# A decoder layer in split fp32: moving the streamed operands to the low end of the partition and the weights to its top

## The chip, the cores and the metric

One core of one Trainium2 chip runs the whole kernel. The metric is device microseconds of one execution. The profile is of one execution of the kernel before; its times are in microseconds from the first instruction.

In the profile PE is TensorE's matmuls, PEld its weight loads, DVE is VectorE, ACT is ScalarE, POOL is GpSimd and SP is SyncE, which issues most DMAs. A matmul's **stationary** operand (128×128 here) is loaded into the array first; its **moving** operand (128×512 here) is then streamed through it. A row such as `pj<-u,w_hi` names the result, then the moving operand, then the stationary one. SBUF has 224 KiB in each partition, and a tile's **place** is where its bytes begin in every partition, counted from the low end.

## The reference, cut to what is computed

```python
def layer(x, c, positions, ...):                 # x [1, 1024, 1024], d_model 1024, fp32
    mod = silu(c) @ w_ada + b_ada                # six vectors: shift, scale, gate, twice
    u = x * (1 + scale_m) + shift_m
    qa, ka, va, qb, kb, vb, ga, gb = split(u @ w_in)     # w_in is 1024 x 7936
    ya = window_attention(rope(qa), rope(ka), va, sinks) @ w_branch_a   # 16 heads, 2 kv heads
    yb = dilated_attention(rope(qb), rope(kb), vb)       @ w_branch_b   # 3 dilations x 8 heads
    y = (sigmoid(ga) * ya + sigmoid(gb) * yb) @ w_o
    x = layer_norm(2**0.25 * x + (1 + gate_m) * y)
    v = x * (1 + scale_f) + shift_f
    g, h = split(v @ w_gate_up)                  # d_ff 2816
    return layer_norm(2**0.25 * x + (1 + gate_f) * ((silu(g) * h) @ w_down))
```

## The kernel before, in words

**Arithmetic.** Each fp32 operand of the large products is held as two exact parts, high and low. `mac` (L130) makes one product of a 128×128 weight tile with 512 columns out of three matmuls: `w_hi` with the high part (L131), `w_hi` with the low part (L132), `w_lo` with the high part (L133). `matmul(ps, w, m)` takes the stationary operand first and the moving one second.

**Weights.** The class `Weights` streams them in pieces of 512 columns through the pool `wpool` (L98): a DMA into `w_raw`, sometimes a scale, then ACT makes `w_hi` (L72) and DVE `w_lo` (L73). Some pieces go into tiles of their own instead (`pair_dest`, L167): the second half of the output projection (`late`, tiles `o_hl` of pool `opar`) and the down projection (`wd` in pool `ffn`, the last one `wdl` in pool `last`). `split` (L110) does the same to an array: ACT makes the high part (L111), DVE the low part (L112).

**Stages, in the order of the program.** A manual schedule keeps the order in which the program is written as the issue order on each engine.

1. 0 to 70 us: the adaLN vectors, `u`^T (in `bigu`, eight tiles of 8 KiB), the rope's tables, and the first three projections, whose stationary operands are tiles `e_hi` and `e_lo` of the pool `pro` (`first_macs`, L271 and L276).
2. 70 to 828 us: the other projections `pj<-u,w` into which the attention is woven. `rotary` (L406) turns a projection: DVE L415 makes `ra`, L416 `rb`, L419 the sum into a tile `o` for queries and `r` for keys; `q_stacks` makes `qs` from `o` (L432 and L433), `k_stacks` makes `kh` and `kl`. Scores are L497, transposes of the probabilities L535, the sums with the values L556, and their result is copied into a tile `o` by ACT (L558). Pool `att` holds all of these; `o` has four buffers for queries and for results. The results of window attention are scaled (L607) and stored to DRAM (`oa_d`, L608); for the last pair of heads (p=7) both are done by POOL (`side`, L601), for the others by DVE and SP.
3. 828 to 1120 us: for two branches of four pairs of heads from `w_branch_a` and one from `w_branch_b`, the gate `p<-u,w` and the product `p<-o_hl,w`. `o_parts` (L788) reads back the stored heads, four tiles a branch: SP loads `o_raw` (L784, two buffers) and `split` makes `o_hl` (four buffers in `opar`).
4. 1120 to 1230 us: the output projection from the merged array `m` (in `bigu` again): `p<-w,m` for the first half of the features with `m` stationary, `pf<-o_hl,m` for the second half, whose weights are the `late` tiles. Then a layer norm and the FFN's input `v` (`ffn_input`, L996): token half t=0 in the pool `u2p` (L988), t=1 in `bigu`.
5. 1230 to 1960 us: the FFN, in groups of two columns of 128: `pf<-v,w` for gate and up, `h` in `bigu`, and `pd<-wd,h` with `h` stationary and `wd` moving.
6. The last layer norm and the stores.

**Places.** A pool takes its space from the low end, or from the top with `side="right"`, and gives it back when it closes. A tile that comes to lie where earlier tiles lay waits for everything that wrote or read them; this is how a place becomes a wait, on the engine that first writes the new tile.

Of the kernel before, what the change touches and what calls it, by code (L numbers as in the profile page):

```python
# [10 lines left out]
F32 = mybir.dt.float32  # L11
# [7 lines left out]
P = 128  # L19
# [21 lines left out]
class Weights:  # L41
    """Streams weights in pieces of 512 columns: DMA, an optional scale, and two exact parts."""
# [15 lines left out]
    def step(self):  # L58
        """Splits the next piece and sends for the one that fits behind it."""
        i = len(self.done)  # L60
        if i >= len(self.jobs):
            return
        self.send()
        _, kh, scale, dest = self.jobs[i]
        raw = self.raws.pop(i)
        if scale is not None:
            self.nc.gpsimd.tensor_tensor(raw, raw, scale(), op=OP.mult)  # L67
        if dest is None:
            hi, lo = [self.pool.tile([P, 512], F32R, name=s, tag=s, bufs=4) for s in ("w_hi", "w_lo")]
        else:  # L70
            hi, lo = dest()
        self.nc.scalar.activation(hi, raw, AF.Copy)  # L72
        self.nc.vector.tensor_tensor(lo, raw, hi, op=OP.subtract)  # L73
        self.done.append((hi, lo, kh))
        self.send()

    def prepare(self, pieces):
        """Sees to it that the next pieces are split."""
        while len(self.done) < min(self.used + pieces, len(self.jobs)):
            self.step()  # L80

    def take(self, pieces):
        """The next pieces, as a function from the chunk to its two parts."""
        self.prepare(pieces)
        got = self.done[self.used:self.used + pieces]
        self.used += pieces
        kh = got[0][2]
        n = 512 // kh
        return lambda k: [got[k // kh][s][:, (k % kh) * n:(k % kh + 1) * n] for s in range(2)]
# [3 lines left out]
def decoder_layer(ctx: ExitStack, tc: tile.TileContext, I, out, dbg=None):  # L93
# [4 lines left out]
    wpool = ctx.enter_context(tc.tile_pool(name="wpool", bufs=2))  # L98
# [15 lines left out]
    # silu(c), one value per partition and chunk of the contraction  # L114
# [6 lines left out]
    def wide(name, pool, halves=(0, 1)):  # L121
        """A [128, 8, 1024] array in two exact parts: a function of part, token half and chunk."""
        ts = {(s, t, k): pool.tile([P, 4, TH], F32R, name=f"{name}{s}{t}{k}", tag="big")
              for t in halves for k in range(2) for s in range(2)}
        return lambda s, t, k: ts[s, t, k // 4][:, k % 4]
# [41 lines left out]
    def pair_dest(store, key, pool, name, bufs):  # L167
        def dest():
            if key not in store:
                store[key] = [pools[pool].tile([P, 2, D], F32R, name=name, bufs=bufs), 0]  # L170
            hl, c = store[key]
            store[key][1] += 1
            return hl[:, 0, c * 512:(c + 1) * 512], hl[:, 1, c * 512:(c + 1) * 512]
        return dest

    for eh in range(2):
        for kp in range(4):
            add_chunk(I["w_o"][eh, kp], 2, 1, lambda eh=eh: gates[2][:, eh * 512:(eh + 1) * 512],
                      pair_dest(late, kp, "opar", "o_hl", 4) if eh else None)
    for f in range(NF):  # L180
        add_chunk(I["w_gate_up"][f], 2, 4)
        add_chunk(I["w_gate_up"][NF + f], 2, 4)
        for c in range(2):
            ws.add(I["w_down"][f * P:(f + 1) * P, c * 512:(c + 1) * 512], 1,
                   lambda c=c: gates[5][:, c * 512:(c + 1) * 512],
                   pair_dest(wd_t, f, "ffn", "wd", 3) if f < NF - 1 else pair_dest(wd_t, f, "last", "wdl", 1))
# [23 lines left out]
    early = {}  # L210
    with tc.tile_pool(name="pro", bufs=2) as pro:
# [14 lines left out]
        # shift and scale of all the chunks, as columns of one bank  # L226
        ps_m = ps_t.tile([P, TH], F32, name="pt")

        def ada_sum(j):
            """Products of the adaLN weights with silu(c), summed over the later chunks."""  # L230
            acc_t[j] = pro.tile([P, 2 * P], F32, name="acc", bufs=2)
            k0 = on_pe[j]
            nc.vector.tensor_scalar(acc_t[j], wa_t[j][:, k0], c_act[:, k0:k0 + 1], None, op0=OP.mult)
            for k in range(k0 + 1, KC):
                nc.vector.scalar_tensor_tensor(acc_t[j], wa_t[j][:, k], c_act[:, k:k + 1], acc_t[j],
                                               op0=OP.mult, op1=OP.add)
# [27 lines left out]
        def first_macs(j):  # L264
            """What the j-th chunk of u^T brings to the first projections, in pieces."""
# [18 lines left out]
        def table_steps():  # L284
            """The rope's angles, reduced to [-pi, pi] (cosines as sines of a quarter turn less the angle's size)."""
# [68 lines left out]

    att = ph1.enter_context(tc.tile_pool(name="att", bufs=2, side="right", reuse_waits="tile"))
    mask_a, mask_b = mask[:, 0:3:2], mask[:, 1:3]

# [44 lines left out]
    def residue_half(ap, r, t):  # L402
        """The places of token half t in an array ordered by the residue modulo r."""
        jn = TH // r
        return ap.rearrange("p (r j) -> p r j", r=r)[:, :, t * jn:(t + 1) * jn]

    def rotary(e, r, then):
        """Rotated features, tokens in the order of their residue modulo r."""
        res = att.tile([P, T], F32, name="o", bufs=4) if e == 2 else att.tile([P, T], F32, name="r", bufs=1)
# [17 lines left out]
    def q_stacks(e, r, box):  # L427
        """Per head [q_hi; q_lo], the leading part on the head's own partitions."""
        def stack(res, h):
            own, other = ((LO, HI), (HI, LO))[h]  # L430
            q = att.tile([P, T], F32R, name="qs", bufs=4)
            nc.scalar.activation(q[own], res[own], AF.Copy)  # L432
            nc.vector.tensor_tensor(q[other], res[own], q[own], op=OP.subtract)  # L433
            box.setdefault("q", []).append(q)
# [7 lines left out]
    def k_stacks(e, r, both, box):  # L442
        """Per head [k_hi; k_hi] and k_lo, on the head's own partitions or on both halves."""
        def stack(res, h):
            own, other = ((LO, HI), (HI, LO))[h]
            kh = att.tile([P, T], F32R, name="kh", bufs=4)
# [18 lines left out]
    def values(e, r, box):  # L465
        """Values [key in block, block, feature], tokens in the order of their residue modulo r."""
# [17 lines left out]
    def scores(un, half, h):  # L484
        """Scaled and masked scores of four blocks of a head, and their maxima, negated."""
# [53 lines left out]
    def weigh(un, half):  # L539
        """Sums of the values for four blocks of both heads."""  # L540
# [9 lines left out]
        if half == 0:  # L550
            un["o"] = att.tile([P, T], F32, name="o", bufs=4)
# [25 lines left out]
    def keep_sums(un):  # L577
        """The reciprocal sums of A's exponentials, the sinks' among them."""
# [22 lines left out]
    def side(p):  # L601
        """The last pair's end keeps to the engine that has nothing else to do then."""
        return (nc.gpsimd, nc.gpsimd) if p == A_PAIRS - 1 else (nc.sync, nc.vector)
# [95 lines left out]
    def tasks(n, i):  # L699
        """What follows the attention of earlier units."""  # L700
# [63 lines left out]
    zp = ctx.enter_context(tc.tile_pool(name="zp", bufs=2, reuse_waits="tile"))  # L764
    misc = ctx.enter_context(tc.tile_pool(name="misc", bufs=1, reuse_waits="tile"))
    ph2, ph2b = ExitStack(), ExitStack()
    opar = ph2.enter_context(tc.tile_pool(name="opar", bufs=4, side="right", reuse_waits="tile"))
    pools["opar"] = opar
# [19 lines left out]
    def o_parts(b):  # L788
        parts = []
        for k in range(4):  # L790
            send_parts(4 * b + 4)
            hl = opar.tile([P, 2, T], F32R, name="o_hl")
# [122 lines left out]
    def moments(tb):  # L915
        """The mean and, still as a variance, the scale of each row."""
# [7 lines left out]
    def norm_quick(tb, gb, dst=None):  # L924
        """z = (z - mean) * gain / sigma + bias for each row of z [128, 1024]."""
# [9 lines left out]
    def norm_shared(tb, gb, dst):  # L935
        """The same with the work spread over three engines, the end as a function to call later."""
# [51 lines left out]
    u2p = ctx.enter_context(tc.tile_pool(name="u2p", bufs=4, reuse_waits="tile"))  # L988
# [7 lines left out]
    def ffn_input(t, dc):  # L996
        if t not in u2:
            u2[t] = wide("v", u2p if t == 0 else bigu, (t,))
# [34 lines left out]
    ph2.close()  # L1033
# [4 lines left out]
    groups = [2] * 9 + [4]  # L1038
    ffn = ctx.enter_context(tc.tile_pool(name="ffn", bufs=2, side="right", reuse_waits="tile"))
    pools["ffn"] = ffn  # L1040
# [11 lines left out]
    for gi, n in enumerate(groups):  # L1052
# [3 lines left out]
        for f in fs:  # L1056
            h = bigu.tile([P, 2, T], F32R, name="h", tag="big")
# [16 lines left out]
            if f == 0:  # L1074
# [5 lines left out]
                pools["last"] = ctx.enter_context(tc.tile_pool(name="last", bufs=1, reuse_waits="tile"))  # L1080
# [32 lines left out]
def _layout(a):  # L1113
    """The arrays as the kernel reads them: reordered only."""
# [67 lines left out]
```

## Time and profile before

| what | value |
|---|---|
| three runs | 1974.82, 1977.31 and 1979.35 us, median 1977.31 |
| the profiled execution, first to last instruction | span 1974.0 us; the profile gives no other time of it |
| PE busy | 1925.3 us (98%), 9252 matmuls |
| DVE, ACT, POOL busy | 1088.3 (55%), 678.5 (34%), 390.5 (20%) |
| mean granted TensorE clock | 0.995 |
| PE idle, 0 to 70 us | 17 us |
| PE idle, 70 to 828 us | 12 us |
| PE idle, 828 to 1120 us | 3 us |
| PE idle, 1120 to 1230 us | 2 us |
| PE idle, 1230 to 1960 us | 7 us |
| PE idle, 1960 to 1974 us | 8 us |

The idle times are each stretch less PE's busy time in it. How to read it: matmuls are pipelined, so one matmul's duration (some 390 ns) is longer than the distance from its start to the next one's start (some 230 ns), and it is the distance that adds up to the span. Starts are read from the timeline; the granted clock is 1.00 at full speed.

### The profile page before, as it was taken

How to read it: one execution, taken by the hardware profiler on the slowest of the kernel's cores; microseconds unless marked ns; L12 is line 12 of the kernel's file. 1: busy time of each engine (PE TensorE's matmuls, PEld its weight loads, DVE VectorE, ACT ScalarE, POOL GpSimd, SP SyncE). 2: the span in 40 equal slices, each digit the busy share in tenths (PEclk: the TensorE clock that was granted, in tenths of full speed). 3: DMA queues.
4: the chain of work that ended last, by engine and by line, in shares of the span. 5: the costliest groups of instructions: out<-in, count | busy, mean ns of one | idle time of the engine just before them, and what ended most of it. 6: DMA issues, size and time to landing. Idle time of an engine off the chain costs nothing.

```text
span 1974.0 us, 24286 instructions
## 1 busy us (share of the span) xinstructions
PE 1925.3 (98%) x9252; PEld 1548.0 (78%) x9252; DVE 1088.3 (55%) x2111; ACT 678.5 (34%) x1501; POOL 390.5 (20%) x259
## 2 busy tenths in 40 slices
PE   6899999999999999999999999999999999999998
PEld 5688878878878777778888878787778777877886
DVE  8755567677676877435454558434433343334337
ACT  3555444445445677532121314211121112111222
POOL 2422223323332222001211333000010001000013
PEclk9899999999999999999999999999999999999999
DMA  8011111121121212355442242111111111111112
GB/s 311 22 38 39 36 59 54 39 66 49 34 72 43 89 65 70 126 180 166 160 144 80 62 131 70 54 54 42 39 59 43 43 43 65 38 38 54 54 48 86
DMA packets 68518, 146.16 MB, mean 74 GB/s; under 512 B 12529, under 2 KB 13617, under 8 KB 68402
## 3 DMA queue, kind: packets, MB, share of 16 engines
q1 hardware_dynamic: 68066, 143.56, 22.2%
q8 instruction: 73, 1.20, 0.3%
q0 software_dynamic: 336, 1.06, 0.2%
q14 instruction: 43, 0.35, 0.1%
HBM read 132.69 MB, written 11.89 MB: 73 GB/s over the span
## 4 chain that ended last, share of the span: by engine, by line
PE 84%; DVE 9%; ACT 2%; DMA 2%; issue 2%; POOL 1%; SPq 0%; DVEq 0%; ACTq 0%
PE pf L132 9%; PE pf L131 9%; PE pf L133 9%; PE pj L131 7%; PE pj L133 7%; PE pj L132 7%; PE p L132 5%; PE p L133 5%; PE p L131 5%; PE pd L131 4%; PE pd L133 4%; PE pd L132 4%; PE s L497 3%; PE pt L535 2%; PE po L556 2%
## 5 line engine op out<-in xcount | busy, mean ns | idle before, releaser
L131 PE MATMUL pj<-u,w_hi 128*128 128x512 f32 x720 | 300.8, 418 | 0.0
L73 DVE TENSOR_TENSOR w_lo<-w_raw,w_hi 128x512 fp32r<-128x512 f32 x238 | 198.9, 845 | 174.9 <-ACT w_hi L72 171.8
L133 PE MATMUL pj<-u,w_lo 128*128 128x512 f32 x720 | 283.3, 393 | 0.0
L132 PE MATMUL pj<-u,w_hi 128*128 128x512 f32 x720 | 282.0, 392 | 0.0
L131 PE MATMUL pf<-v,w_hi 128*128 128x512 f32 x704 | 276.5, 393 | 0.0
L132 PE MATMUL pf<-v,w_hi 128*128 128x512 f32 x704 | 276.2, 392 | 0.0
L133 PE MATMUL pf<-v,w_lo 128*128 128x512 f32 x704 | 275.7, 392 | 0.0
L67 POOL TENSOR_TENSOR w_raw<-w_raw,gate 128x512 f32<-128x512 f32 x60 | 81.8, 1369 | 637.6 <-DMA w_raw<-in_w_down 436.2
L418 POOL TENSOR_TENSOR rb<-rb,sin_t 128x512 f32<-128x512 f32 x64 | 86.9, 1357 | 510.3 <-DVE rb L416 359.7
L519 ACT ACTIVATE probs<-probs,st 128x128 f32<-128x128 f32 (+1 forms) x320 | 146.0, 460 | 53.6 <-DVE st L513 26.6
L1096 DVE SCALAR_TENSOR_TENSOR zt<-zt,pd 128x512 f32<-128x512 f32 x160 | 109.3, 688 | 99.4 <-PE pd L133 99.4
L131 PEld LDWEIGHTS pj<-u,w_hi 128*128 128x128 f32 x720 | 135.9, 189 | 33.5 <-issue 4.9
L133 PEld LDWEIGHTS pj<-u,w_lo 128*128 128x128 f32 x720 | 135.5, 188 | 30.7
L1068 ACT ACTIVATE sg<-pf 128x512 f32<-128x512 f32 x44 | 26.3, 597 | 384.2 <-PE pf L133 384.2
L131 PEld LDWEIGHTS pf<-v,w_hi 128*128 128x128 f32 x704 | 131.9, 187 | 30.2
L133 PEld LDWEIGHTS pf<-v,w_lo 128*128 128x128 f32 x704 | 131.9, 187 | 30.2
L72 ACT ACTIVATE w_hi<-w_raw 128x512 fp32r<-128x512 f32 x238 | 144.5, 622 | 32.0 <-PE p L132 12.5
L132 PEld LDWEIGHTS pf<-v,w_hi 128*128 128x128 f32 x704 | 132.0, 187 | 29.8
L132 PEld LDWEIGHTS pj<-u,w_hi 128*128 128x128 f32 x720 | 136.2, 189 | 22.4
L131 PE MATMUL pd<-wd,h 128*128 128x512 f32 x336 | 133.5, 397 | 6.7 <-DVE zt L1096 6.7
L133 PE MATMUL pd<-wd,h 128*128 128x512 f32 x336 | 133.2, 396 | 0.0
L132 PE MATMUL pd<-wd,h 128*128 128x512 f32 x336 | 132.6, 395 | 0.0
(211 smaller groups left out, 3303.8 us busy)
## 6 DMA issues: line engine op xcount, KB each, us to landing
w_raw<-in_w_in SPq DMA_DIRECT2D x118, 256.0 KB
w_raw<-in_w_gate_up SPq DMA_DIRECT2D x88, 256.0 KB
a_raw<-in_w_ada SPq DMA_DIRECT2D x32, 512.0 KB
w_raw<-in_w_down SPq DMA_DIRECT2D x44, 256.0 KB
wa<-in_w_ada_m SPq DMA_DIRECT2D x16, 512.0 KB
wb<-wt_d SPq DMA_DIRECT2D x24, 256.0 KB
xt<-in_xT SPq DMA_DIRECT2D x8, 512.0 KB
w_raw<-in_w_branch_a SPq DMA_DIRECT2D x16, 256.0 KB
```

What stands on the lines that cost most here:

```text
L67: self.nc.gpsimd.tensor_tensor(raw, raw, scale(), op=OP.mult)
L72: self.nc.scalar.activation(hi, raw, AF.Copy)
L73: self.nc.vector.tensor_tensor(lo, raw, hi, op=OP.subtract)
L131: nc.tensor.matmul(ps, w[0], m[0], start=first, stop=False)
L132: nc.tensor.matmul(ps, w[0], m[1], start=False, stop=False)
L133: nc.tensor.matmul(ps, w[1], m[0], start=False, stop=last)
L418: eng.tensor_tensor(b, b, sin_t[:, s], op=OP.mult)
L497: nc.tensor.matmul(pss[i // 2][:, i % 2, lo:], lhs[:, b * P:(b + 1) * P], rhs[:, (b - 1 + lo) * P:(b + 1) * P], start=first and i % 2 == 0 ...
L519: nc.scalar.activation(pr, pr, AF.Exp, bias=st[:, 0, h, b:b + 1], accum_out=st[:, 1, h, b:b + 1])
L535: nc.tensor.transpose(pt[:, i, :], probs[:, b - 4 * half, int(kb == b)], ident)
L556: nc.tensor.matmul(po[(LO, HI)[h], c0:c0 + n * P], v[:, kb, c * 64:(c + 1) * 64], pts[h][:, i:i + n, :], start=(ji == 0), stop=(ji == len( ...
L1096: nc.vector.scalar_tensor_tensor(z, z, ALPHA if gi == 0 else 1.0, pd, op0=OP.mult, op1=OP.add)
```

## The change

The order of the instructions on every engine stays as it was. What moves is where tiles lie, and with that what some instructions wait for. In `after` the scratch for DMA descriptors at the low end of the partition shrinks from 16 KiB to 2 KiB; `wpool`, `zp` and `misc` go to the top; the tiles `o`, `kh` and `qs` leave `att` for a pool `attl` at the low end; the tiles `o_hl`, `late`, `wd` and the last `h` share five slots of 8 KiB in a pool `low`, which takes the place of `attl` once that has closed; both halves of `v` go into `bigu`; and `h` gets three slots of its own in `ffn`.

Places in KiB from the low end of the partition, taken from the two built programs:

| tile | role on PE | before | after |
|---|---|---|---|
| DMA scratch | none | 0 to 16 | 0 to 2 |
| `u`, `m` | `u` moving, `m` stationary | 39.4 to 103.4 | 3.4 to 67.4 |
| `v`, t=0 | moving | 151.8 to 183.8 | 3.4 to 67.4, both halves |
| `v`, t=1 | moving | 39.4 to 103.4 | as above |
| `w_hi`, `w_lo` | stationary; moving in `p<-w,m` | 23.4 to 39.4 | 208 to 224 |
| `e_hi`, `e_lo` | stationary | 165.5 to 189.5 | 129.5 to 153.5 |
| `o_hl`, `late`, `wd` | moving | 192 to 224 | 67.4 to 107.4 |
| `h` | stationary | 47.4 to 79.4 | 125.5 to 149.5 |
| attention's `o`, `kh`, `qs` | `kh`, `qs` in the scores | 128 to 184 | 67.4 to 115.4 |
| `zt` (fp32 state) | transposed only | 103.4 to 135.4 | 170 to 202 |
| `ra`, `rb`, `r`, `vt`, `v` of attention | `v` in the sums | 104 to 131 | `ra` 134 to 138, the others nearby |

Two places show what becomes of the waits. On ACT, where stage 3 begins: the last copies of attention's results (`o<-po`), two weight splits, and the four `o_hl` splits of the first branch. Names such as `DMASW3_49` are semaphores, one for each engine or DMA queue. Before:

```order
L558 ACTIVATE o<-po 128x512 [waits PE_49]
L582 ACTIVATE es<-st,sinks 128x8 x2
L664 ACTIVATE r<-pj 128x512 [waits PE_49]
L72 ACTIVATE w_hi<-w_raw 128x512 [waits DMAHW6_49]
L72 ACTIVATE w_hi<-w_raw 128x512 [waits DMAHW1_49]
L111 ACTIVATE o_hl<-o_raw 128x1024 [waits DMAHW0_49,Activation_49]
L111 ACTIVATE o_hl<-o_raw 128x1024 [waits DMAHW1_49,Activation_49]
L111 ACTIVATE o_hl<-o_raw 128x1024 [waits DMAHW5_49,DMAHW7_49,DMAHW4_49,PE_49]
L111 ACTIVATE o_hl<-o_raw 128x1024 [waits DMAHW3_49,DMAHW2_49,DMAHW5_49,DMASW0_49,DVE_49]
L664 ACTIVATE gt<-p_7761 128x512 [waits PE_49]
```

And after:

```order
L560 ACTIVATE o<-po 128x512 [waits PE_49]
L584 ACTIVATE es<-st,sinks 128x8 x2
L666 ACTIVATE r<-pj 128x512 [waits PE_49]
L72 ACTIVATE w_hi<-w_raw 128x512 [waits DMAHW6_49]
L72 ACTIVATE w_hi<-w_raw 128x512 [waits DMAHW1_49]
L111 ACTIVATE o_hl<-o_raw 128x1024 [waits DMAHW0_49,DMAHW7_49,DMASW3_49,Pool_49]
L111 ACTIVATE o_hl<-o_raw 128x1024 [waits DMAHW1_49]
L111 ACTIVATE o_hl<-o_raw 128x1024 [waits DMAHW4_49]
L111 ACTIVATE o_hl<-o_raw 128x1024 [waits DMAHW5_49]
L666 ACTIVATE gt<-p_7765 128x512 [waits PE_49]
```

The instructions are the same. The first split now lies over slots 0 and 1 of attention's `o`, and the tile in slot 0 is that of the last pair, p=7: so it waits for POOL's scale of that tile (`Pool_49`, L607 of before) and for POOL's DMA that stores it (`DMASW3_49`, L608).

On DVE, the first rope after stage 1. Before:

```order
L73 TENSOR_TENSOR w_lo<-w_raw,w_hi 128x512 [waits DMAHW1_49,Activation_49]
L415 TENSOR_TENSOR ra<-pj,cos_t 128x512 [waits DMAHW2_49,PE_49]
L416 STREAM_SHUFFLE rb<-pj 128x512
L415 TENSOR_TENSOR ra<-pj,cos_t 128x512 [waits PE_49]
L416 STREAM_SHUFFLE rb<-pj 128x512
```

And after:

```order
L73 TENSOR_TENSOR w_lo<-w_raw,w_hi 128x512 [waits DMAHW1_49,Activation_49]
L417 TENSOR_TENSOR ra<-pj,cos_t 128x512 [waits PE_49]
L418 STREAM_SHUFFLE rb<-pj 128x512
L417 TENSOR_TENSOR ra<-pj,cos_t 128x512
L418 STREAM_SHUFFLE rb<-pj 128x512
```

Here too the order is the same. `ra` (134 to 138 KiB) now lies over `e_hi` (129.5 to 141.5), so the first row's count on `PE_49` is that of the last matmul that reads `e_hi`; the third and later rows then need no PE count of their own.

The diff, without the removed comments:

```diff
-    wpool = ctx.enter_context(tc.tile_pool(name="wpool", bufs=2))
+    wpool = ctx.enter_context(tc.tile_pool(name="wpool", bufs=2, side="right"))
...
-    def pair_dest(store, key, pool, name, bufs):
+    def pair_dest(store, key, pool, name):
...
-                store[key] = [pools[pool].tile([P, 2, D], F32R, name=name, bufs=bufs), 0]
+                store[key] = [pools[pool].tile([P, 2, D], F32R, name=name, tag="big"), 0]
...
-                      pair_dest(late, kp, "opar", "o_hl", 4) if eh else None)
+                      pair_dest(late, kp, "low", "o_hl") if eh else None)
...
-                   pair_dest(wd_t, f, "ffn", "wd", 3) if f < NF - 1 else pair_dest(wd_t, f, "last", "wdl", 1))
+                   pair_dest(wd_t, f, "low", "wd"))
...
+    attl = ph1.enter_context(tc.tile_pool(name="attl", bufs=4, reuse_waits="tile"))
     att = ph1.enter_context(tc.tile_pool(name="att", bufs=2, side="right", reuse_waits="tile"))
...
-        res = att.tile([P, T], F32, name="o", bufs=4) if e == 2 else att.tile([P, T], F32, name="r", bufs=1)
+        res = attl.tile([P, T], F32, name="o", bufs=4) if e == 2 else att.tile([P, T], F32, name="r", bufs=1)
...
-            q = att.tile([P, T], F32R, name="qs", bufs=4)
+            q = attl.tile([P, T], F32R, name="qs", bufs=4)
...
-            kh = att.tile([P, T], F32R, name="kh", bufs=4)
+            kh = attl.tile([P, T], F32R, name="kh", bufs=4)
...
-            un["o"] = att.tile([P, T], F32, name="o", bufs=4)
+            un["o"] = attl.tile([P, T], F32, name="o", bufs=4)
...
-    zp = ctx.enter_context(tc.tile_pool(name="zp", bufs=2, reuse_waits="tile"))
-    misc = ctx.enter_context(tc.tile_pool(name="misc", bufs=1, reuse_waits="tile"))
-    ph2, ph2b = ExitStack(), ExitStack()
-    opar = ph2.enter_context(tc.tile_pool(name="opar", bufs=4, side="right", reuse_waits="tile"))
-    pools["opar"] = opar
+    zp = ctx.enter_context(tc.tile_pool(name="zp", bufs=2, side="right", reuse_waits="tile"))
+    misc = ctx.enter_context(tc.tile_pool(name="misc", bufs=1, side="right", reuse_waits="tile"))
+    pools["low"] = low = ctx.enter_context(tc.tile_pool(name="low", bufs=5, reuse_waits="tile"))
+    ph2b = ExitStack()
...
-            hl = opar.tile([P, 2, T], F32R, name="o_hl")
+            hl = low.tile([P, 2, T], F32R, name="o_hl", tag="big")
...
-    u2p = ctx.enter_context(tc.tile_pool(name="u2p", bufs=4, reuse_waits="tile"))
...
-            u2[t] = wide("v", u2p if t == 0 else bigu, (t,))
+            u2[t] = wide("v", bigu, (t,))
...
-            h = bigu.tile([P, 2, T], F32R, name="h", tag="big")
+            h = (ffn if f < NF - 1 else low).tile([P, 2, T], F32R, name="h", tag="big", bufs=3 if f < NF - 1 else 5)
...
-    nc = bacc.Bacc("TRN2", target_bir_lowering=False, num_devices=1)
+    nc = bacc.Bacc("TRN2", target_bir_lowering=False, num_devices=1, dynamic_dma_scratch_size=2048)
```

More of the change, by code (lines that the diff above doesn't have):

```diff
@@ L1032, in decoder_layer @@
             nc.sync.dma_start(dbg["x1"][tb * P:(tb + 1) * P], zrow(tb))
-    ph2.close()
     if dbg.get("stop") == 2:
@@ L1039, in decoder_layer @@
     ffn = ctx.enter_context(tc.tile_pool(name="ffn", bufs=2, side="right", reuse_waits="tile"))
-    pools["ffn"] = ffn
     gb2 = norm_params(2)
@@ L1079, in decoder_layer @@
                 x2_ctx.close()
-                pools["last"] = ctx.enter_context(tc.tile_pool(name="last", bufs=1, reuse_waits="tile"))
             else:
```

## The prediction

> **What bounds the kernel now.** I read the page first, for the span and the busy engines, then the chain that ended last.
>
> ```profile
> span 1974.0 us, 24286 instructions
> PE 1925.3 (98%) x9252; PEld 1548.0 (78%) x9252; DVE 1088.3 (55%) x2111; ACT 678.5 (34%) x1501; POOL 390.5 (20%) x259
> PE 84%; DVE 9%; ACT 2%; DMA 2%; issue 2%; POOL 1%; SPq 0%; DVEq 0%; ACTq 0%
> ```
>
> PE is busy for 98% of the span and carries 84% of the chain. So two things can move the time by much: the distance from one matmul's start to the next, over thousands of them, and new gaps on PE. A change of places touches both. Next I read the groups of instructions by form, for the counts. Each product appears in three lines (L131, L132, L133) of the same count, so these rows are multiplied by three.
>
> ```profile
> L131 PE MATMUL pj<-u,w_hi 128*128 128x512 f32 x720 | 300.8, 418 | 0.0
> L131 PE MATMUL pf<-v,w_hi 128*128 128x512 f32 x704 | 276.5, 393 | 0.0
> L131 PE MATMUL pd<-wd,h 128*128 128x512 f32 x336 | 133.5, 397 | 6.7 <-DVE zt L1096 6.7
> L131 PE MATMUL p<-u,w_hi 128*128 128x512 f32 x224 | 88.5, 395 | 0.0
> L132 PE MATMUL p<-o_hl,w_hi 128*128 128x512 f32 x192 | 76.3, 397 | 1.4 <-DVE o_hl L112 1.4
> L131 PE MATMUL pf<-o_hl,m 128*128 128x512 f32 x64 | 26.0, 407 | 1.2 <-DVE zt L967 1.2
> L131 PE MATMUL p<-w_hi,m 128*128 128x512 f32 x64 | 24.9, 389 | 0.0
> ```
>
> That is 2160 matmuls of pj, 2112 of pf from v (1056 for each token half), 1008 of pd, 672 of p from u, 576 of p from o_hl, 192 each of the last two. Durations overlap, so the price has to be read from starts, in the timeline of PE, where no row waits. First the FFN, at the step from token half t=0 (v high in the partition, 152 KiB and up) to t=1 (v low, 39 to 103 KiB):
>
> ```profile
> 1494.62 0.39 PE L131 MATMUL pf<-v,w_hi 128*128 128x512 f32 x1
> ...
> 1500.21 0.39 PE L131 MATMUL pf<-v,w_hi 128*128 128x512 f32 x1
> ...
> 1502.05 0.39 PE L133 MATMUL pf<-v,w_lo 128*128 128x512 f32 x1
> ...
> 1505.67 0.39 PE L131 MATMUL pf<-v,w_hi 128*128 128x512 f32 x1
> ```
>
> The first two rows are 24 matmuls apart: 5.59 us, 232.9 ns each. The next 24 take 5.46 us, 227.5 ns each, and the last 16 of them 3.62 us, 226.3 ns. The weights (23 to 39 KiB) and the form are the same; only the moving operand's place differs. High costs some 6.5 ns a matmul. A second case, the branch's product with o_hl at 192 KiB and up as the moving operand:
>
> ```profile
> 851.97 0.39 PE L131 MATMUL p<-o_hl,w_hi 128*128 128x512 f32 x1
> ...
> 859.67 0.39 PE L131 MATMUL p<-o_hl,w_hi 128*128 128x512 f32 x1
> ```
>
> 33 apart: 233.3 ns. So far this speaks for the change. But the change also sends every weight to 208 KiB and up. Has any matmul of before a high stationary operand and a low moving one? Only those of the first stage, with e_hi and e_lo at 165 to 190 KiB and u low. The window there and the rows:
>
> ```profile
> 62.00:68.00 6.00, 6.00 (x27) 4.81 (x27) 1.90 (x3) 2.87 (x5) 1.29 (x1) 1.00 0.26 84
> ```
>
> ```profile
> 61.82 0.40 PE L271 MATMUL pj<-u,e_hi 128*128 128x512 f32 x1
> ...
> 66.97 0.39 PE L271 MATMUL s<-u,e_hi 128*128 128x512 f32 x1
> ...
> 70.25 0.39 PE L131 MATMUL pj<-u,w_hi 128*128 128x512 f32 x1
> ...
> 72.74 0.39 PE L133 MATMUL pj<-u,w_lo 128*128 128x512 f32 x1
> ```
>
> PE never idles there and its clock is 1.00. From 61.82 to 66.97 there are 22 matmuls, 234.1 ns each; from 61.82 to 70.25 36, 234.2 ns. At 70.25 the stationary operand changes to w_hi at 23 KiB, with u where it was, and the next 11 take 226.4 ns each. The price of a high stationary operand is as large as that of a high moving one, and it starts at the very matmul at which the place changes.
>
> **The change part by part.** The prices are 226.4 with both operands low, 233.3 with the moving one high, 234.2 with the stationary one high. I have no row with both high, and after has none that I count.
>
> 1. pj goes from both low to stationary high. Inside the weave its base is not 226.4, since the matmuls just behind transposes are slower:
>
> ```profile
> 340.81 0.39 PE L132 MATMUL pj<-u,w_hi 128*128 128x512 f32 x1
> ...
> 343.10 0.39 PE L133 MATMUL pj<-u,w_lo 128*128 128x512 f32 x1
> ```
>
> Ten apart, 229.0 ns. Whether that loss stays on top of 234.2 or is swallowed by it no row shows. I take it as swallowed: 2160 × (234.2 − 229.0) = +11.2 us; on top of it would be 2160 × 7.8 = +16.8.
> 2. p from u, the same without transposes: 672 × 7.8 = +5.2.
> 3. pf, t=1, the same from 227.5: 1056 × 6.7 = +7.1.
> 4. p from w and m: there the weight is the moving operand, now high, and m stationary and low: 192 × (233.3 − 226.4) = +1.3.
> 5. The operands that get low streams also get high weights. pf, t=0, goes from 232.9 to 234.2: 1056 × 1.3 = +1.4. p from o_hl: 576 × 0.9 = +0.5. pd, with h at 125 to 149 KiB, a place between those I have rows for: 1056 with the last wd's, × 0.9 = +1.0; if that place counts as low, 1056 × −6.9 = −7.3.
> 6. pf from o_hl and m gets both operands low: 192 × −6.9 = −1.3.
>
> Sum of the places: 11.2 + 5.2 + 7.1 + 1.3 + 1.4 + 0.5 + 1.0 − 1.3 = **+26.4 us**, from 18 (h counted as low) to 32 (the loss behind transposes on top).
>
> 7. The new wait of ACT's first o_hl split (L111) on POOL's scale and store of the last pair. The timelines of ACT, DVE, POOL and PE:
>
> ```profile
> 834.62 1.06 ACT L111 ACTIVATE o_hl<-o_raw 128x1024 fp32r<-128x1024 f32 x1 [5.39 <-DMA o_raw<-oa_d]
> ```
>
> ```profile
> 845.23 1.23 DVE L112 TENSOR_TENSOR o_hl<-o_raw,o_hl 128x1024 fp32r<-128x1024 f32 x1 [1.09 <-ACT o_hl L111]
> ```
>
> ```profile
> 840.14 2.37 POOL L607 TENSOR_TENSOR o<-o,vt 128x1024 f32<-128x1024 f32 x1 [3.65 <-DMA vt<-wa_d]
> 842.81 0.60 POOL L608 DMA_DIRECT2D oa_d<-o  x1 [0.30 <-POOL o L607]
> ```
>
> ```profile
> DMA to landing us min/median/max: 5.9/5.9/5.9
> ```
>
> ```profile
> 838.65 0.40 PE L131 MATMUL p<-o_hl,w_hi 128*128 128x512 f32 x1
> ...
> 846.51 0.50 PE L132 MATMUL p<-o_hl,w_hi 128*128 128x512 f32 x1 [0.65 <-DVE o_hl L112]
> ```
>
> Today the split starts at 834.62. The store is issued at 842.81 and lands 5.9 us later (the row of oa_d's store from POOL's queue), at 848.7; from then on only may the split write. That is 14.1 us later. Behind it on ACT stand the other three splits, the gate's tanh and the weight splits; behind those the low parts on DVE, and behind the low part the next two o_raw loads on SP, since o_raw has two buffers. The fourth low part ended at 846.46 and PE took it at 846.51. The same chain of 11.8 us from the first split now ends at 848.7 + 11.8 = 860.5. PE has nothing else to do: its gate is done at 838.65, and the next gate stands behind this product. **+14.0 us**, from 10 (if the splits run closer, since the loads have long landed) to 14.5.
> 8. The new wait of DVE's first rope:
>
> ```profile
> 68.34 0.69 DVE L415 TENSOR_TENSOR ra<-pj,cos_t 128x512 f32<-128x512 f32 x1 [2.55 <-PE pj L276]
> ```
>
> ```profile
> 85.45 4.26 DVE L433 TENSOR_TENSOR qs<-o,qs 64x1024 fp32r<-64x1024 f32 x2
> ```
>
> ```profile
> 69.78 0.63 PE L276 MATMUL po<-u,e_hi 128*128 128x512 f32 x2
> ...
> 81.86 0.39 PE L133 MATMUL pj<-u,w_lo 128*128 128x512 f32 x1
> ...
> 88.52 1.23 PE L497 MATMUL s<-kh,qs 128*128 128x128 f32 x4 [6.27 <-DVE qs L433]
> ```
>
> It ran at 68.34, once pj was complete; now it must wait for the last reader of e_hi, which ends at 69.78 + 0.63 = 70.41. DVE then works without a gap up to qs, for which PE waits at 88.52. **+2.1 us**, and no less than 0.
> 9. A gap of over 10 us on PE also costs clock, as this one does:
>
> ```profile
> 84.00:88.00 4.00, 0.00 (x0) 0.00 (x0) 3.94 (x3) 0.00 (x0) 2.51 (x1) 0.57 0.21 66
> 88.00:92.00 4.00, 3.48 (x11) 2.85 (x12) 3.92 (x10) 0.00 (x0) 0.86 (x1) 0.50 0.00 0
> 92.00:96.00 4.00, 4.00 (x14) 3.13 (x13) 2.63 (x6) 2.29 (x9) 2.56 (x2) 0.65 0.00 0
> ```
>
> After the idle time from 82 to 88.5 the clock stands at 0.50 for 88 to 92 and 0.65 for 92 to 96, some 3 us of full clock lost. In stage 3 most of that would fall between 849 and 860, where PE is short of work in any case: **+1**, from 0 to 3. [...]
> 10. The other waits that move (h with three slots, the five shared slots, v in bigu) fall on tiles whose last readers are done earlier, and cost nothing: PE is the engine that reads them, and the next writer is at least one group of the FFN behind. If h's third slot did bind, it would be in the FFN's only idle time, 6.7 us before pd. [...]
>
> Sum: 26.4 + 14.0 + 2.1 + 1 = 43.5. On the execution's own 1974.0 that is 2017.5. The median is 3.3 above that span, and the page has no other time of this execution; I carry the 3.3 over: **2021 us**.
>
> **The rivals.** *Only the moving operand's place counts.* For it: the two moving cases above are clean, and the first stage has a form of its own (L271). Against it: the step from 234.2 to 226.4 at 70.25. It would give pf t=0, p from o_hl, pd and pf from o_hl their 6.6 to 6.9 ns back, 2880 × 6.7 = −19.3, +1.3 for p from w, and the stalls stay: −18 + 17.1 = −0.9, so 1976, no change. It decides when the start distance of pj in after is still below 230.
>
> *The same without ACT's wait.* This is the other side: the store lands before PE is short of work, or the wait doesn't hold the split. Then −18 + 2 = −16, 1961. Against it stands that ACT's order is fixed and 842.81 is POOL's own issue.
>
> *Places count for nothing,* and the distances above have other causes, such as the instructions around them. Then only the waits are left: +17.1, 1994. [...] The trace disagrees, with 226.3 against 232.9 ns in one loop, so I give it little.
>
> *The wait is hidden and places count as I say:* 43.5 − 15 = +28.5, 2006; inside my range.
>
> **How the numbers follow.** Both operands count: 0.76, with the wait or, in 0.05 of it, without; 2021. Only the moving one: 0.13 with the wait, 0.04 without. Places count for nothing: 0.07. The range reaches down to the last, less 2 us, 1992, and up to 2021 + 5.6 (losses behind transposes on top) + 2 (clock) + 4 for what no row prices, 2032; that leaves out the 0.17 of the second rival. A difference of 0.2%, 4 us, is about what can be told from no change. Faster takes the 0.04 and a quarter of the 0.13: 0.07. Same takes most of the rest of that: 0.09. Slower has 0.84.
>
> **What would show it.** Right: the timeline of PE shows pj at 234 ns from start to start and pf alike for both token halves; ACT's first o_hl split starts at about 14 us behind the gate with a wait named after oa_d's store; PE idles about 14 us before that product. Wrong: pj at 227 to 230 (only streams count), pf t=0 unchanged from t=1 and both at 226 to 227; a split that starts with its o_raw; or h at 125 KiB and up letting pd run at 227.

## The result and the profile after

The changed kernel takes 2005.59 us (median of 4 runs, 2005.14 to 2006.74) where before takes 1977.44: a ratio of 1.0147, 95% interval 1.0133 to 1.0162. It is 28 us slower; the forecast was 2021, with a range of 1992 to 2032. The profiled execution grew by 29.7 us, from 1974.0 to 2003.7:

```profile
span 2003.7 us, 24280 instructions
PE 1947.4 (97%) x9252; PEld 1551.8 (77%) x9252; DVE 1081.2 (54%) x2111; ACT 679.0 (34%) x1501; POOL 390.0 (19%) x259
```

PE does the same 9252 matmuls, is busy 22 us longer, and waits 8 us longer. Both matter below. First the distances between starts, in the timeline of PE, for pj within the weave and for pf over both token halves:

```profile
348.64 0.40 PE L132 MATMUL pj<-u,w_hi 128*128 128x512 f32 x1
...
350.28 0.39 PE L133 MATMUL pj<-u,w_lo 128*128 128x512 f32 x1
...
1529.81 0.40 PE L132 MATMUL pf<-v,w_hi 128*128 128x512 f32 x1
...
1544.80 0.40 PE L133 MATMUL pf<-v,w_lo 128*128 128x512 f32 x1
```

Seven matmuls of pj take 1.64 us, 234.3 ns each, and 64 of pf 14.99 us, 234.2 ns each; the step between the two token halves is gone. Next, the start of the branches, in ACT's, POOL's and PE's timelines, the landing of oa_d's store from POOL's queue, and windows over the gap (columns: us, busy time of PE, PEld, DVE, ACT and POOL, granted clock, DMA share, GB/s):

```profile
854.22 2.00 ACT L111 ACTIVATE o_hl<-o_raw 128x1024 fp32r<-128x1024 f32 x2 [17.27 <-DMA oa_d<-o]
```

```profile
851.20 0.60 POOL L610 DMA_DIRECT2D oa_d<-o  x1 [0.30 <-POOL o L609]
```

```profile
DMA to landing us min/median/max: 2.9/2.9/2.9
```

```profile
846.44 0.40 PE L133 MATMUL p<-u,w_lo 128*128 128x512 f32 x1
855.33 0.79 PE L131 MATMUL p<-o_hl,w_hi 128*128 128x512 f32 x1 [8.49 <-ACT o_hl L111]
...
865.20 0.50 PE L132 MATMUL p<-o_hl,w_hi 128*128 128x512 f32 x1 [0.76 <-DVE o_hl L112]
```

```profile
847.00:855.00 8.00, 0.00 (x0) 0.00 (x0) 0.00 (x0) 0.78 (x1) 2.94 (x2) 0.68 0.17 67
855.00:860.00 5.00, 4.21 (x9) 3.02 (x10) 2.36 (x2) 1.22 (x2) 0.00 (x0) 0.50 0.45 132
```

As forecast, ACT waits for the store of the last pair, for 17 us here; PE stands still from 847 to 855, and the clock is at 0.50 until 860. And in the first stage:

```profile
70.23 0.69 DVE L417 TENSOR_TENSOR ra<-pj,cos_t 128x512 f32<-128x512 f32 x1 [4.67 <-PE po L276]
```

```profile
71.71 0.47 PE L131 MATMUL pj<-u,w_hi 128*128 128x512 f32 x1 [1.52 <-DVE rb L418]
```

The rope waits for the last reader of `e_hi`. PE pays at once, and not first at `qs`: in the row above it is released by `rb` (L418) after 1.52 us, since the next projection is written to a buffer of `ps_pj` that the rope is still to read.

So far the prediction seems borne out step by step. But the experiments below show that its main mechanism was wrong.

### The profile page after: what moved, and what is told of

Its sections match the earlier page's. It is cut to its first block, busy times and chain, and to the rows that moved or that the text cites. A ratio compares the mean times of both kernels' runs of the same rounds, so it can differ in the third digit from the quotient of the medians.

```text
span 2003.7 us, 24280 instructions
## 1 busy us (share of the span) xinstructions
PE 1947.4 (97%) x9252; PEld 1551.8 (77%) x9252; DVE 1081.2 (54%) x2111; ACT 679.0 (34%) x1501; POOL 390.0 (19%) x259
## 4 chain that ended last, share of the span: by engine, by line
PE 53%; DVE 3%; DMA 1%; ACT 0%; issue 0%; POOL 0%; DVEq 0%; POOLq 0%; ACTq 0%
PE pf L131 9%; PE pf L133 9%; PE pf L132 9%; PE p L132 5%; PE p L133 5%; PE p L131 5%; PE pd L131 4%; PE pd L133 4%; PE pd L132 4%; DVE m L112 1%; DVE h L112 1%; PE px L1001 0%; DVE sg L1068 0%; DVE zt L1093 0%; ACT h L111 0%
## 5 line engine op out<-in xcount | busy, mean ns | idle before, releaser
L131 PE MATMUL pf<-v,w_hi 128*128 128x512 f32 x704 | 279.7, 397 | 0.0
L132 PE MATMUL pf<-v,w_hi 128*128 128x512 f32 x704 | 279.1, 396 | 0.0
L1066 ACT ACTIVATE sg<-pf 128x512 f32<-128x512 f32 x44 | 26.4, 599 | 386.5 <-PE pf L133 386.5
L131 PE MATMUL pd<-wd,h 128*128 128x512 f32 x352 | 139.2, 395 | 4.9 <-DVE zt L1093 4.9
L133 PE MATMUL pd<-wd,h 128*128 128x512 f32 x352 | 139.9, 397 | 0.0
L132 PE MATMUL pd<-wd,h 128*128 128x512 f32 x352 | 138.9, 395 | 0.0
```

The source lines that it names most:

```text
L131: nc.tensor.matmul(ps, w[0], m[0], start=first, stop=False)
L132: nc.tensor.matmul(ps, w[0], m[1], start=False, stop=False)
L133: nc.tensor.matmul(ps, w[1], m[0], start=False, stop=last)
L1066: nc.scalar.activation(sg[t], ps[0, t], AF.Silu)
```

## The experiments

The theory on record was that a place high in the partition costs TensorE some 7 ns a matmul, for either operand. The rivals were that only the moving operand's place counts, and that places count for nothing. Times are medians; each ratio is against the kernel before on the same chip.

**A map of places (e1).** A kernel without the layer: 26 tiles from 6 to 214 KiB, and PE takes each as the stationary and each as the moving operand.

```diff
+    def run(m, s, n):
+        for r in range(n):
+            nc.tensor.matmul(ps[r % 2], w[s][:, 512:640], w[m][:, :512], start=True, stop=True)
+
+    for s in range(NPL):
+        for m in range(NPL):
+            run(m, s, REP)
```

> Computes nothing of the layer: after 26 tiles of 8 KiB are filled, from 6 to 214 KiB, PE runs nine matmuls of 128x128 by 128x512 for each pair of a stationary and a moving tile, 676 pairs, back to back, and the output is zeros. Theory (either operand counts, by a threshold): 226.7 ns from start to start where both lie low, 233 to 234 ns where one lies high, with the threshold between 104 KiB (fast in the kernel before) and 125 KiB for the stationary one (h in the changed kernel took 233.3), below 152 KiB for the moving one; both high as one high, about 234. Rival 1 (the two prices add): both high 241. Rival 2 (the distance between the two operands counts): fast along the diagonal at every place, slow in both corners, and no threshold. Rival 3 (the form or the stage counted and not the place): one number everywhere.

The rows of the stationary operand run from low to high through the span, so windows over it show the map by stationary place; each window goes through the moving places from low to high five to six times:

```profile
100.00:400.00 300.00, 300.00 (x1325) 248.43 (x1324) 0.00 (x0) 0.00 (x0) 0.00 (x0) 1.00 0.00 1
...
1000.00:1300.00 300.00, 300.00 (x1325) 248.39 (x1324) 0.00 (x0) 0.00 (x0) 0.00 (x0) 1.00 0.00 1
```

1325 matmuls in 300 us, 226.4 ns each, with low and with high weights. By the starts, all 676 pairs lie between 226.6 and 226.8 ns. In this map a place costs nothing. This was the outcome of rival 3 of that expectation, and it leaves a question: what was the 7 ns in the kernel, if not the place?

**The weights alone at the top (e2).**

```diff
-    wpool = ctx.enter_context(tc.tile_pool(name="wpool", bufs=2))
+    wpool = ctx.enter_context(tc.tile_pool(name="wpool", bufs=2, side="right"))
```

> The kernel before with the weight pool alone at the top of the partition; the streams and the waits stay as they were. Theory (a high stationary operand costs 7 ns): pj +7.5 us as the changed kernel shows it, p from u +4.4, pf of the second token half +7, p from w and m +1.2 since there the weight streams; the products whose stream is high already go to both high, by one price together +2: +22, about 1999 us. Rival (only the moving operand counts): +1.2, the same time as before, 1978.

With the weights gone from the low end, the streams there move 22 KiB down. 1990.03 us, ratio 1.0076 (1.0061 to 1.0091), between the two forecasts. pj, p from u, pf and p from w and m lose 7.6, 4.4, 7.3 and 1.2 us, by the sums of their start distances, just as forecast. But the waits shrink by some 4 us, 1.7 of them in front of pd, and one product gets faster, by 3.4 us: p from o_hl, stream and weights both high, in PE's timeline:

```profile
879.97 0.39 PE L131 MATMUL p<-o_hl,w_hi 128*128 128x512 f32 x1
...
889.03 0.39 PE L132 MATMUL p<-o_hl,w_hi 128*128 128x512 f32 x1
```

Forty apart, 226.5 ns each, where before took 233.3. Meanwhile pf of the first token half, also with both high (from 130 KiB and from 208 KiB), stays at 233.7. Two products with both operands high, one fast and one slow: neither the places nor their sum explains it. What differs is the addresses' low bits. Call an address modulo 256 its residue, and two operands with the same residue alike. In e2 the weights have residue 224 and o_hl has 224, but v has 64. The kernel before fits this too. There u, w, h and m at the low end have residue 128, o_hl and wd at the top 224, e_hi and e_lo, behind small tiles, 224, and v of t=0, behind other small tiles, 64: in its undisturbed rows like and like is 226.3 and 226.4 ns, unlike 232.9 to 234.2. Places and residues had changed together, since the side of a pool and the small tiles ahead of it set both.

**The changed kernel with low weights (e3).**

```diff
-    wpool = ctx.enter_context(tc.tile_pool(name="wpool", bufs=2, side="right"))
+    wpool = ctx.enter_context(tc.tile_pool(name="wpool", bufs=2))
```

> The changed kernel with the weight pool alone back at the low end. Theory: pj -7.7 us, p from u -4.4, pf of both token halves -15, p from o_hl -4, p from w and m -1.2, ACT's wait for the store stays: -32 from 2005.6, about 1973, just below the kernel before. Rival (only the moving operand counts): -1.2, 2004.

1976.73 us, ratio 1.0006 (0.9996 to 1.0015). The weights' place, or something that goes with it, is worth 28 us here; the rival that only the moving operand counts is out. pj gives back 8.2 us, pf 15.5, p from u 4.8, p from o_hl 4.2. The shortfall against −32 is in waits, among them +2.2 us in front of pd and +1.2 in the attention. With weights at residue 128 this run speaks for residues as well as for places; it can't separate them.

**Without the wait for the store (e4).**

```diff
-            un["o"] = attl.tile([P, T], F32, name="o", bufs=4)
+            last = un.get("a") == A_PAIRS - 1
+            un["o"] = att.tile([P, T], F32, name="cst", bufs=1) if last else attl.tile([P, T], F32, name="o", bufs=4)
```

> The changed kernel with the last pair's attention result in the tile cst of the pool att, so that the first o_hl split does not lie over it. Theory: the split starts with its own o_raw some 7 us behind where it started before, PE waits some 4 us there in place of 13 and keeps its clock: -11 us, about 1994.5. Rival (another wait, of the low parts or the o_raw loads, ends just as late): 2004 to 2006.

1995.71 us, ratio 1.0099 (1.0084 to 1.0114). ACT's timeline and windows as above:

```profile
843.45 1.06 ACT L111 ACTIVATE o_hl<-o_raw 128x1024 fp32r<-128x1024 f32 x1 [5.47 <-DMA o_raw<-oa_d]
```

```profile
847.00:855.00 8.00, 6.13 (x24) 4.36 (x23) 3.01 (x5) 3.61 (x5) 2.97 (x2) 0.95 0.98 330
850.73:854.14 3.41, 1.60 (x6) 1.12 (x7) 2.07 (x2) 2.93 (x5) 1.29 (x2) 1.00 0.92 356
854.14:857.55 3.41, 3.41 (x10) 2.60 (x9) 3.41 (x6) 1.39 (x4) 0.00 (x0) 0.50 0.37 138
```

The split now waits for its own o_raw, and PE works through most of 847 to 855. The theory that the clock holds was wrong in part: behind a stretch in which PE was busy for 1.60 of 3.41 us it is at 0.50 from 854.1 to 857.6. By the starts the place gives back 10.3 us. The wait is shown, and no other took its place.

**A map of offsets (e5).** As e1, with two low tiles and the two operands shifted within them by 16 offsets each, from 0 to 1024 bytes.

```diff
+    for so in OFF:
+        for mo in OFF:
+            run("xs", [so], "xm", mo, REP)
```

> Computes nothing of the layer: PE runs 13 matmuls of 128x128 by 128x512 for each pair of 16 byte offsets, from 0 to 1024, of the stationary and of the moving operand, both tiles low and 8 KiB apart; the output is zeros. New theory (what counts is whether the two operands' addresses are the same modulo some power of two, not where they lie): 226.7 ns on the diagonal and wherever the offsets differ by a multiple of the modulus, 233 to 234 ns elsewhere. The four kernels so far show a difference of 0 modulo 256 as fast and of 96, 160 and 192 modulo 256 as slow, so the modulus is 128 or more, if the theory holds. Rival 1 (each operand's own alignment counts): slow rows and columns, with no fast diagonal off the aligned ones. Rival 2 (places count, and the map of places was fast for another reason, such as zeros as data): 226.7 everywhere. Besides, sections for bf16, for plain fp32 and for 128, 256 and 384 columns, of which nothing is expected.

Mean ns from start to start of 11 gaps a pair, worked out from the trace; rows are the stationary operand's offset in bytes, columns the moving one's (both tiles begin at residue 128; of the 16 offsets, those that are multiples of 32 up to 256 are shown, without the rows 160 and 224):

```
          0    32    64    96   128   160   192   224   256
    0 226.6 233.5 229.4 233.5 233.7 233.6 233.0 232.8 226.6
   32 233.2 226.7 233.5 229.4 233.5 233.7 233.5 232.9 232.9
   64 233.1 233.2 228.5 233.4 229.4 233.5 233.7 233.6 233.0
   96 234.4 233.4 232.9 226.7 233.5 229.4 233.5 233.6 233.5
  128 233.0 233.7 232.7 232.8 226.7 233.5 229.4 233.5 233.7
  192 229.2 234.5 233.0 234.5 233.3 232.8 226.6 233.5 229.5
  256 226.6 233.5 229.4 233.5 233.7 233.5 232.9 232.9 226.6
```

The diagonal is fast and comes back at 256; off it, the price is about 7 ns (233.5 against 226.6), but only 2.8 (229.4) where the moving operand is 64 bytes ahead. The 228.5 at 64 is no price but a slow start. The pairs follow each other without a break, and a like pair behind an unlike one needs up to ten matmuls to reach its pace. All twelve gaps of two like pairs, in ns (offset of the stationary operand, then of the moving one):

```
 64,  64   230 236 228 233 231 226 227 227 226 227 227 226
  0, 512   239 233 236 224 231 236 228 232 231 227 227 226
```

All 29 like pairs at multiples of 32 bytes, up to 1024, end at 226 to 227 ns, and none of the 140 unlike ones does. So it is the difference of the two addresses that counts, modulo 256. Each operand's own alignment (rival 1) is out for multiples of 32 bytes, and so is rival 2: the operands are zeros here, and the price is there.

**The changed kernel with like residues (e6).**

```diff
+    padr = ctx.enter_context(tc.tile_pool(name="padr", bufs=1, side="right"))
...
+    nc.gpsimd.memset(padr.tile([P, 24], F32, name="pad"), 0.0)
...
-            mod = pro.tile([P, 2], F32, name="mod", bufs=3)
+            mod = pro.tile([P, 2], F32, name="mod", bufs=8)
...
-        rs = misc.tile([P, 2], F32, name="brs", bufs=3)
+        rs = misc.tile([P, 2], F32, name="brs", bufs=5)
```

> The changed kernel with every tile at its place to within 256 bytes: 96 bytes of padding at the top and a few more small buffers bring the address of every fp32r operand to 128 modulo 256; weights stay at the top, streams low, and ACT's wait for the store stays. New theory: all products at 226.7 ns, pj -7.7 us, p from u -4.4, pf -15.3, p from w and m -1.2, p from o_hl -4.1, pd -6.6: about 1966. Theory of the prediction (places count): no change, 2005.

1969.48 us, ratio 0.9964 (0.9951 to 0.9976): 36 us less than the changed kernel, by shifts of less than 256 bytes. PE's timeline (its lines stand two lower here), pd and then pf:

```profile
1490.04 0.39 PE L135 MATMUL pd<-wd,h 128*128 128x512 f32 x1
...
1496.84 0.39 PE L135 MATMUL pd<-wd,h 128*128 128x512 f32 x1
1497.06 0.39 PE L133 MATMUL pf<-v,w_hi 128*128 128x512 f32 x1
...
1499.33 0.39 PE L134 MATMUL pf<-v,w_hi 128*128 128x512 f32 x1
```

Thirty of pd at 226.7 ns and ten of pf at 227, with weights at the top and streams low. The products gain 41 us by their start distances, where 39 was forecast; waits, 2.2 us of them in front of pd, take some 5 back, so it is 1969 and not 1966. The theory of the prediction, no change, has fallen.

**The kernel before with like residues (e7).** The same edit to the kernel before.

> The kernel before with the same padding and nothing else: places to within 256 bytes and all waits as they were, every fp32r operand at 128 modulo 256. New theory: pf of the first token half -6.8 us, p from o_hl -3.9, pd -6.9, pf from o_hl and m -1.3: about 1958. Theory of the prediction: no change, 1977.

1958.75 us, ratio 0.9908 (0.9893 to 0.9923). PE's timeline across the two token halves:

```profile
1486.11 0.39 PE L134 MATMUL pf<-v,w_hi 128*128 128x512 f32 x1
...
1499.93 0.39 PE L135 MATMUL pf<-v,w_lo 128*128 128x512 f32 x1
```

61 apart, 226.6 ns, with no step between a v at 152 KiB and one at 39: the very rows on which the prediction was built. pf gained 7.7 us, pd 6.5, p from o_hl 3.9.

**The kernel before, spoiled by 32 bytes (e8).**

```diff
+    padl = ctx.enter_context(tc.tile_pool(name="padl", bufs=1))
     bigu = ctx.enter_context(tc.tile_pool(name="bigu", bufs=8))
...
+    nc.gpsimd.memset(padl.tile([P, 8], F32, name="pad"), 0.0)
```

> The kernel before with 32 bytes of padding between the weight pool and bigu: the weights stay at 23 KiB and u at 39 KiB, but their addresses now differ by 32 modulo 256. New theory: pj +7.7 us, p from u +4.4, pf of the second token half +7, p from w and m +1.2: about 1997, as slow as the change of places was without its waits. Theory of the prediction: both operands are low, no change, 1977.

1984.81 us, ratio 1.0045 (1.0031 to 1.0059). The sign is right, the size is not: +8 and not +20. pj, p from u, pf and p from w and m lost 6.2, 3.8, 6.0 and 1.2 us. But pd won 4 us and pf from o_hl and m 0.7. In PE's timeline:

```profile
1489.66 0.39 PE L135 MATMUL pd<-wd,h 128*128 128x512 f32 x1
...
1500.65 0.39 PE L135 MATMUL pd<-wd,h 128*128 128x512 f32 x1
```

48 apart, 229.0 ns. I had forgotten that h and m move with bigu: wd with residue 224 is now 64 ahead of h with 160, and 64 ahead is the 229.4 of the map. Fewer waits (1.6 us in front of pd, 0.9 in the attention, 0.8 around p from w and m) make up most of the rest.

**Both repairs together (e9).** e6 with the edit of e4.

> The changed kernel with both repairs, the padding of e6 and the last pair's tile of e4: all new places kept, addresses alike modulo 256, no wait for the store. If residues and the two waits are the whole account, it stands at the aligned kernel before (1958.8) plus the rope's wait of 1.5 to 2 us: about 1960.5. Rival (the places still cost something by themselves): 1964 or more. Second rival (low streams bring something of their own): 1956 or less.

1960.09 us, ratio 0.9921 (0.9908 to 0.9935). This is 1.3 us above e7, and the rope's wait alone would be 1.5 to 2. So the places of the change, with like residues and without its wait for the store, cost or bring nothing that these runs can tell; each of the two intervals reaches some 3 us to either side.

**The small DMA scratch alone (e10).**

```diff
-    nc = bacc.Bacc("TRN2", target_bir_lowering=False, num_devices=1)
+    nc = bacc.Bacc("TRN2", target_bir_lowering=False, num_devices=1, dynamic_dma_scratch_size=2048)
```

> The kernel before with the DMA scratch alone at 2 KiB, which moves every tile from the low end down by 14 KiB, a multiple of 256 bytes. New theory: residues stay, so no change, 1977 within 2 us. Rival (POOL's few DMAs suffer from the small scratch): slower where the last pair's store ends late, by up to 3 us.

1975.79 us, ratio 0.9994 (0.9985 to 1.0003): no change.

**Like residues for the attention too (e11).** e7 with small paddings and a few more buffers (`b_pp`, `c_act`, `sinks`, `es`, `mx`, `st`), and the small scratch, which makes room.

> The aligned kernel before (e7), in which the operands of the transposes, the scores and the sums with the values now also lie alike modulo 256 (room for that from the DMA scratch at 2 KiB). In e7 the projections woven into the attention still take 229.6 ns from start to start, 226.7 in undisturbed stretches. Theory (the slower matmuls behind a transpose are left over from its operands' unlike addresses): 1913 x 2.9 = -5.5 us, about 1953. Rival (they come from the change of form or size, or from the engines' hand-over): 1958.8, as e7.

1959.21 us, ratio 0.991 (0.9895 to 0.9925), as e7. The woven pj went from 229.6 to 229.2 ns only, so the slower matmuls behind transposes don't come from the addresses of the attention's operands. They run through the slow start that e5 shows. PE's timeline of e11 behind a transpose:

```profile
160.65 0.39 PE L134 MATMUL pj<-u,w_hi 128*128 128x512 f32 x1
...
162.03 0.39 PE L134 MATMUL pj<-u,w_hi 128*128 128x512 f32 x1
...
162.94 0.39 PE L135 MATMUL pj<-u,w_lo 128*128 128x512 f32 x1
```

The six gaps between the first two of these rows are 224 231 236 228 233 231 ns, and the four behind them 226 227 227 226. The first nine of these ten are, to within 1 ns, the last nine of the pair 0, 512 above. Over all of e11 the second to fourth gap behind another form is 231.3 to 232.8 ns on average, the eleventh 226.9. Whether the other form sets it off or the hand-over between engines, and why the start has this shape, is open.

## Why the prediction was right, and where it was wrong

The sign, the time within its range, and both waits were right; the mechanism under the largest term was not, and that the time came out all the same was luck. The account of the 29.7 us, from the distances of all starts in the two traces (a gap of over 0.3 us, among them starts 0.43 us apart at a granted clock of 0.50, counts as a wait and is kept apart):

| term | forecast, us | measured, us | moving less stationary address, modulo 256: before, after | ns before, after |
|---|---|---|---|---|
| pj | +11.2 | +7.7 | 0, 160 | 229.7, 233.8 |
| p from u | +5.2 | +4.4 | 0, 160 | 227.6, 234.3 |
| pf, both halves | +8.5 | +8.1 | 192 and 0, 160 | 230.3, 234.3 |
| p from w and m | +1.3 | +1.2 | 0, 96 | 227.0, 233.4 |
| p from o_hl | +0.5 | +0.4 | 96, 160 | 233.6, 234.3 |
| pd | +1.0 | −0.2 | 96, 96 | 233.5, 233.3 |
| pf from o_hl and m | −1.3 | −0.9 | 96, 0 | 233.2, 228.1 |
| ACT's wait, with the clock | +15.0 | +10.7 | | |
| rope's wait | +2.1 | +1.7 | | |
| waits that shrank (pd −1.9, attention −1.5) | 0 | −3.4 | | |
| sum | 43.5 | 29.7 | | |

**The wrong step** is "High costs some 6.5 ns a matmul" and, after it, "The price of a high stationary operand is as large as that of a high moving one". Both observations were clean, but each compared two tiles that differed in two things, the place and the address modulo 256. The "very matmul at which the place changes" was also the one at which the residue changes, from 224 to 128. That e1 is flat, that e2 has a fast and a slow product with both operands high, and that e6 and e7 win 36 and 18 us by shifts under 256 bytes decides it. What in the chip makes the difference of addresses count, no run shows. The sum of the places came out nearly right, 20.7 us for 26.4, since the residues happened to change with the places: pj, p from u, pf of the second half and p from w and m went from like to unlike, pf from o_hl and m from unlike to like. The signs that the prediction named for being right came too (pj at 234 ns, pf the same in both halves, the split behind the store), because none of them tells a place from an address. Nor does the time: 2006 was also given to the case with the wait hidden, and it was not hidden. The table shows how well the difference of addresses orders all rows: the only fast ones are those at 0.

**Step 1** mis-sized pj: 4.1 ns each and not 5.2, and only on the 1915 of its starts that follow without a wait. That the loss behind transposes is swallowed was right.

**Step 7** had the wait, its place and its releaser right; the size was off. The store landed 2.9 us after its issue, where 5.9 was carried over from before, and with both o_raw there the first two splits ran back to back, in 2.00 us; so +10.7 in place of 15. e4 confirms it by taking it away. The clock stayed at 0.50 for about 5 us after the gap, until 860.1. As step 9 had it, most of that cost nothing by itself: back at full clock (0.99 from 860 to 864), PE still waited 0.3 to 0.8 us for each of the later splits and low parts, up to the fourth.

**Step 8** had +2.1 where +1.7 was measured, but by another path, through PE's wait for `rb` (1.52 us) and not for `qs`.

**Step 10** took every other wait as unmoved. With a slower pf, zt is ready sooner in front of pd, which gave 1.9 us back; e2 and e8, which also slow pf, gave back 1.7 and 1.6 us there.

Of the 15 us from 2021 to the measured time, the two sums account for 13.8. The rest is in the 3.3 us carried over from span to median: the changed kernel's profiled execution took 2005.5 us at a span of 2003.7.

**The rivals.** That places count for nothing was right as a statement on places, and its time was wrong, since addresses do count. In e1 like residues take 226.6 to 226.8 ns at every pair of places; with unlike ones e5 shows 233.5. I had given this rival 0.07 and had not asked what else the step in the rows could be. That only the moving operand counts is refuted by e3.

## What to carry to other kernels

Two tiles that differ in place can differ in their addresses' low bits too, as the two halves of v did here (64 and 128 modulo 256): print both before a difference is put down to either. For fp32r matmuls of 512 columns in this kernel, the moving and the stationary operand should begin at the same address modulo 256 (like pairs end at 226 to 227 ns in e5, the other pairs of its table have means of 229 to 235); the gain found here, 18 us or 0.9%, came from 96 bytes of padding and a few spare buffers, with no tile moved to another end. And a tile placed over an old one inherits that one's last reader or store: ask for the latest of them, here a store issued by POOL, which cost 10.7 us with the clock.

## What was not expected of the hardware

In e5, offsets that are no multiple of 32 bytes follow no such rule: their means are 227 to 240 ns, highest for a moving operand at 4 bytes (236 to 240), and a pair with both at 16 bytes stays at 233.5. A stationary operand that alternates between 0 and 32 bytes, with a moving one at 0, took 232 and 238 in turn, so a like pair among unlike ones is not fast; the changed kernel's last group of the FFN, where like and unlike pairs of pd alternate, shows the same (233.7 for the like ones). Matmuls of 128, 256 and 384 columns showed no price for 32 bytes (112 and 112, 119 and 118, 175 and 173 ns at 0 and 32). Nor did plain fp32, which leaves two records a matmul, 429 ns from record to record at all 16 pairs.

In bf16 most of the 25 pairs have a mean of 215.8 ns and a few 235.5, but those are gaps in the trace and no price. e5's page has fewer matmuls than weight loads there:

```profile
L65 PE MATMUL ps<-bm,bs 128*128 128x512 bf16 x318 | 70.0, 379 | 0.4
L65 PEld LDWEIGHTS <-bs 128*128 128x128 bf16 x325 | 31.7, 98 | 38.3 <-issue 0.2
```

Seven records are missing, 49 places from each other, and each leaves one distance of 431 to 442 ns, about twice 216. The starts of the weight loads, all 325 of them there, are 215 to 217 ns apart from the second on. So in bf16 no pair of offsets from 0 to 256 bytes showed a price (215 to 217 ns).
